# A hybrid decoder layer on one core: the first FFN's norm factor from a row-wise second copy of x

## The chip, the core and the metric

The kernel runs on one core of a Trainium2 chip. The metric is the device time of one execution in microseconds. Four compute engines work side by side, each through its own program in order, and wait for each other on semaphores: TensorE (PE: matmuls into PSUM banks), ScalarE (ACT), VectorE (DVE) and GpSimd (POOL). SyncE (SP) issues most loads, POOL issues the loads that add onto what lies in SBUF already, and both kinds run on the same 16 DMA engines. [...]

## The reference

One layer on x of 512 tokens by 1024 features, fp32: a SwiGLU FFN with RMSNorm, a token mixer, a second FFN, a gated embedding and a last norm. The change touches the norm of the first FFN alone:

```python
def rmsnorm(x, g):
    xf = x.astype(jnp.float32)
    y = xf * lax.rsqrt(jnp.mean(xf * xf, axis=-1, keepdims=True) + EPS)
    return (y * g.astype(jnp.float32)).astype(x.dtype)

h = h + 0.5 * swiglu(rmsnorm(h, ffn1_norm[i]), ffn1_w_gate[i], ffn1_w_up[i], ffn1_w_down[i])
```

The factor `rsqrt(mean(x*x) + EPS)` is one number per token. The kernel multiplies x by the gain alone before the matmuls and applies the factor, called `r`, to the products.

## The kernel before

**Layout and precision.** x is kept with features on partitions: eight tiles `h[d]` of 128 features by 512 tokens. Every fp32 operand is split in two: `hi` is a cast on ACT (L424), `lo` is the operand less `hi` on DVE (L428), and each product takes three matmul passes, hi·hi, hi·lo and lo·hi (L199 to L201, or L624 with 256 columns).

**Steps.** The program is a list of steps. Each has a weight load on SP (`load`, up to six steps ahead), a `split` of that weight two steps ahead, a `product` on PE and `after` work behind the product. `run` walks the list and writes each engine's order; `also(step, what, fn)` appends work at one of these places. Where a step is `urgent`, the `after` work of the step one before comes ahead of the split, otherwise behind it. PE, ACT, DVE and SP keep the order written; POOL's order follows the same text.

**The entry.** Steps 0 and 1 project the layer embedding, and its eight result tiles are stored to DRAM by POOL (L870), two of them pairs in buffers of the tag `rawd`. Steps 2 to 5 are the four plain steps of group 0 of the FFN: "gate, upper", "up, upper", "gate, lower", "up, lower", 24 matmuls of 512 columns each. From step 6 on, groups 1 to 10 use a Strassen-like scheme with seven products of weight and x combinations (steps "1, 7, 2, 6, 4, 5, 3" in group 1, with down-projection steps between them). Its x combinations are made by the class `Early`: `x` forms the scaled x halves and splits them, `t(both, i)` forms combination i in 3, 2, 4 and splits it, `t1` forms the last (subtraction on DVE at L535 into `embt`, cast on ACT at L537, `lo` on POOL at L539). Its weight combinations come from accumulating loads on POOL (L639, L642, L676) and one add on DVE (L634).

**The norm.** `squares` squares each `h[d]` on ACT (L247, L250), POOL adds the eight squares into `ssum` (L251), eight matmuls of one column each against ones sum over partitions into a PSUM bank with tokens on partitions (L261, behind the product of "gate, lower"). On DVE `rsqrt` (L217 to L222) and `diagonals` (L281 to L285) turn the sums into two diagonal matrices, and two matmuls against ones (L298, behind "up, lower") spread the factor over all partitions. ACT keeps the result, `r` (L304), and `plain_gate` multiplies the gate by it (DVE L728) and applies Silu (ACT L729). In group 1, `seed` copies x-products to another bank on ACT (L738), `keep_p7` and `keep_u2` copy banks on ACT (L742, L746), `plain_finish` ends group 0 (DVE L734, L735), and `gate_sum` reads banks on DVE (L756). `behind` hangs three pieces (row sums, factor with spreading, keeping) on three steps:

```python
for step, fn in zip(steps, (sums, spread, lambda: use(self.kept(got["ps"])))):
    also(step, "after", fn)
```

Where the pieces of the entry hang before the change:

```python
also(steps[1], "split", lambda: Early.x(early, 0))
also(steps[3], "split", lambda: (squares(0, 1), Early.x(early, 1), squares(2, 3)))
also(steps[4], "split", lambda: (Early.t(early, 3), squares(4, 5, 6, 7), store_embedding()))
also(steps[6], "split", lambda: Early.t(early, 2))
```

At step 7 come the Silu table load, the forming of combination 4 and `t1`, at step 9 the split of combination 4.

Of the kernel before, what the change touches and what calls it, by code (L numbers as in the profile page):

```python
# [26 lines left out]
AF = mybir.ActivationFunctionType  # L27
ALU = mybir.AluOpType

P = 128  # L30
T = 512
NC = T // P
D = 1024
# [1 line left out]
FF = 2816  # L35
NF = FF // P

G_PARTS = (1, 2, 2, 2, 2, 2)
HT = T // 2
NP = ND // 2  # L40

# [42 lines left out]
def layer_kernel(ctx: ExitStack, tc: tile.TileContext, a: dict, out: bass.AP):  # L84
    nc = tc.nc
# [69 lines left out]
    vec_warm = sb("warm", (P, 1))  # L155
    ones = sb("ones", (P, P))
# [6 lines left out]
    ps = sm_ps()  # L163
# [70 lines left out]
    class Norm:  # L234
# [77 lines left out]
        def behind(self, steps, n, use):  # L312
# [11 lines left out]
            for step, fn in zip(steps, (sums, spread, lambda: use(self.kept(got["ps"])))):  # L324
                also(step, "after", fn)


    class Step:

# [52 lines left out]
    def also(step, what, fn):  # L382

        if what == "after":
            old = step.after[0] if step.after else lambda: None
            step.after = (lambda: (old(), fn()),) + tuple(step.after[1:])
        else:
            old = getattr(step, what) or (lambda: None)
            setattr(step, what, lambda: (old(), fn()))
# [205 lines left out]
    class Group:  # L595


        def __init__(self, src, xfs, shared, j):
            self.src, self.xfs, self.shared, self.j = src, xfs, shared, j
            self.last = j == sum(G_PARTS) - 1  # L600
            self.g = self.hi = None
            self.w11, self.w12, self.w21, self.w22 = (
                Parts(tag) for tag in ("rawb", "rawb", "raw", "raw")
            )
            self.ps = {}
# [81 lines left out]
            s.from_right = i in (1, 2, 7)  # L687
            return s

        def plain_steps(self):  # L690


            def step(w, i, which, lower):
                w_parts = {}

                def split():
                    w_parts[0] = w.split()

                def product():
                    whi, wlo = w_parts[0]  # L700
                    if not lower:
                        self.ps[which] = (
                            [sm_ps(), sm_ps()] if which == "gate" else [bank("mm", 3), acc_ps()]
                        )
                    for m, ps in enumerate(self.ps[which]):
                        for p, xf in enumerate(self.xfs):
                            c = slice((2 * p + m) * P, (2 * p + m + 1) * P)
                            t = (xf.a, xf.b)[lower]
                            passes(
                                by_half(ps), whi[:, c], wlo[:, c], t[:, 0:2, 0], t[:, 0:2, 1],  # L710
                                not lower and p == 0, lower and p == len(self.xfs) - 1,
                            )

                s = Step(product, lambda: self.load((w, i)), None, split, urgent=lower)
                s.from_right = w is self.w12
                return s

            return [
                step(*s) for s in (
                    (self.w21, 2, "gate", False), (self.w11, 0, "up", False), (self.w22, 3, "gate", True), (self.w12, 1, "up", True),  # L720
                )
            ]
# [65 lines left out]
    def swiglu(name, xfs, norm, closed, after, at):  # L788


        shared = {}
        out_norm = Norm()
        src = a[f"{name}_gu"]
        groups = [Group(src[j], xfs, shared, j) for j in range(sum(G_PARTS))]
        gs = [g.steps() if g.j else None for g in groups]

        def down(part, gs_, i, n, last):

            nf = 2 * len(gs_)
            w = Parts("rawd")  # L800
            ds = D_ORDER[i * n : (i + 1) * n]
            ps = {}

            def product(gs_=gs_, first=0, end=None):
                end = len(gs_) if end is None else end
                x = [t for g in gs_[first:end] for t in g.out]
                for k, d in enumerate(ds):
                    if first == 0:
                        ps[d] = sm_ps()
                    accumulate(  # L810
                        ps[d], (w.hi, w.lo), k * nf + 2 * first, x, first == 0, end == len(gs_)
                    )

            def add():
                for d in ds:
                    nc.vector.scalar_tensor_tensor(h[d], ps[d], 0.5, h[d], ALU.mult, ALU.add)  # L816
                if last:
                    for d in ds:
                        after(d)

            def add_norm():
                if last:
                    for d in ds:
                        out_norm.add(h[d])

            step = Step(
                product, lambda: w.load(a[f"{name}_down_{part}"][:, i], n * nf * P), None,
                lambda: w.split(x="x" if (i == 1 if last else part + i) else ""), (add, add_norm),
            )
            if last and i == 0:  # L830
                step.product = lambda: product(end=len(gs_) - 1)
                step.rest = lambda: product(first=len(gs_) - 1)
            return step

        steps = groups[0].plain_steps()
        g0, pending = 0, []
        for part, n in enumerate(G_PARTS):
            if part:
                for j in range(g0, g0 + n):

                    here = pending[: -(-len(pending) // (g0 + n - j))]
                    pending = pending[len(here) :]
                    for i in (1, 7, 2, 6, 4, 5, 3) if j == 1 else (1, 7, 6, 4, 5, 2, 3):
                        steps.append(gs[j][i])
                        if i in ((5, 3 if at else 4) if j == 1 else (7, 5)):
                            steps.append(here.pop(0))
            g0 += n
            last = part == len(G_PARTS) - 1
            each = 2
            mine = groups[g0 - n : g0]  # L850
            pending = [down(part, mine, i, each, last) for i in range(ND // each)]
        steps += pending


        norm.behind(steps[at:], D, lambda r: (shared.update(r=r), groups[0].plain_gate()))
        if at:
            also(steps[8], "split", groups[0].plain_finish)
        else:
            also(steps[3], "after", groups[0].plain_finish)
        also(steps[6 if at else 4], "after", lambda: groups[0].parts_of_g(slice(0, 2)))  # L860
        also(gs[-1][3], "after", closed)
        return steps, out_norm
# [5 lines left out]
    def store_embedding():  # L868
        for to, t in stores:
            nc.gpsimd.dma_start(to, t)  # L870
# [47 lines left out]
    h = [sb("h") for _ in range(ND)]  # L918
    pad(base, "sb")
    x_ffn1, x_mix = [], []  # L920

    ffn1_norm = Norm()
    steps, mix_norm = swiglu(
        "ffn1", x_ffn1, ffn1_norm, lambda: open_region("left", "mix_left"),
        splitter("mix_norm", x_mix), 1,
# [1 line left out]
    steps = [embedding(q) for q in range(2)] + steps  # L927
    for d in range(NP):
        XForms(x_ffn1)
    early = [Early(x_ffn1[d].both_a, x_ffn1[d].both_b, d, "ffn1_norm") for d in (0, 2)]  # L930

    def load_x(*ds):
        for d in ds:
            nc.sync.dma_start(h[d], a["x"][:, d, :])

    def squares(*ds):
        for d in ds:
            ffn1_norm.add(h[d])

    also(steps[1], "load", lambda: load_x(0, 1, 2, 3))  # L940
    also(steps[3], "load", lambda: load_x(4, 5, 6, 7))

    also(steps[1], "split", lambda: Early.x(early, 0))
    also(steps[3], "split", lambda: (squares(0, 1), Early.x(early, 1), squares(2, 3)))
    also(steps[4], "split", lambda: (Early.t(early, 3), squares(4, 5, 6, 7), store_embedding()))
    also(steps[6], "split", lambda: Early.t(early, 2))

    also(
        steps[7], "split",
        lambda: (  # L950
            nc.scalar.activation(vec_warm, ones[:, 0:1], AF.Silu), Early.form(early, 4), Early.t1(early),
        ),
    )
    also(steps[9], "split", lambda: Early.t(early, 4, True))
    ffn1_steps = steps


# [3 lines left out]
    x = x_mix  # L961
# [743 lines left out]
def _laid_out(i):  # L1705
# [5 lines left out]
    def feature_major(m):  # L1711
        return np.ascontiguousarray(m.T.reshape(-1, P, m.shape[0]).transpose(1, 0, 2))

    def units(w):
# [5 lines left out]
    o = {  # L1720
        "x": feature_major(one["x"][0]),
        "p": feature_major(one["p"][0]),
    }
    cols = []
    for name, w in _VECS:
# [18 lines left out]
    for n in ("ffn1", "ffn2"):  # L1744
        o[f"{n}_gu"] = blocks(one[f"{n}_w_up"], one[f"{n}_w_gate"])
        d = units(one[f"{n}_w_down"]).reshape(ND, P, NF, P)[list(D_ORDER)]
        f0 = 0
        for q, g in enumerate(G_PARTS):
            nf = 2 * g
            o[f"{n}_down_{q}"] = np.ascontiguousarray(  # L1750
                d[:, :, f0 : f0 + nf].reshape(ND // 2, 2, P, nf * P).transpose(2, 0, 1, 3).reshape(P, ND // 2, -1)
            )
            f0 += nf
# [39 lines left out]
```

## Time and profile before

| | us |
|---|---|
| median of 3 runs (lowest, highest) | 1093.42 (1093.2, 1093.77) |
| the profiled execution | 1094.19 |
| its span | 1092.5 |
| granted clock of TensorE, mean | 0.996 |

The profile's page gives busy time by engine, and further views give the waits of an engine (waiting line, what ended the wait, total, times, longest), the timeline (start, duration, engine, line, operation, output and inputs) and windows (busy time of PE, weight load, DVE, ACT and POOL, then the granted clock of PE, the busy share of the DMA engines and GB/s). DMA rows give a queue's packets, MB and share of the 16 engines, or an issue's size and the time to its landing. q1 is the queue that SP fills, q0 that of POOL. Times are from the span's start; the first 70 us are the entry.

### The profile page before, as it was taken

What the parts mean: (1) busy time and instruction counts of PE and PEld (TensorE: products, weight loads), DVE (VectorE), ACT (ScalarE), POOL (GpSimd) and SP (SyncE); (2) the same over time, 40 slices, a digit from 0 to 9 for tenths busy, and PEclk for the clock granted to TensorE, in tenths of its full rate; (3) what the DMA queues carried; (4) which work ended last, traced back from release to release, by engine and by line L of the source; (5) the groups of instructions that cost most, each with busy time, mean ns of one, the idle gap of its engine ahead of it and who ended that gap; (6) DMA issues with size and microseconds to landing.
All of it is one profiled execution on the core that took longest, in us unless ns stands there. A gap on an engine that the chain in (4) does not pass through costs nothing.

```text
span 1092.5 us, 16566 instructions
## 1 busy us (share of the span) xinstructions
PE 1073.4 (98%) x6687; PEld 949.0 (87%) x6687; DVE 781.8 (72%) x1078; ACT 520.2 (48%) x715; POOL 153.4 (14%) x139
## 2 busy tenths in 40 slices
PE   9889999999999999999999999999999999999997
PEld 7789999999998788787878888899999999999886
DVE  7797776676667696766987766678766776767766
ACT  6554343444444455474673343454444344344554
POOL 3401000000000300134223000000000000000311
PEclk9999999999999999999999999999999999999999
DMA  9759766675624233444332333567766766643412
GB/s 362 200 140 238 195 154 180 174 193 138 182 50 134 75 93 106 135 136 135 101 112 78 97 97 107 181 155 213 202 156 184 193 179 188 161 129 100 142 50 78
DMA packets 49037, 161.67 MB, mean 148 GB/s; under 512 B 5568, under 2 KB 5824, under 8 KB 48960
## 3 DMA queue, kind: packets, MB, share of 16 engines
q1 hardware_dynamic: 38288, 124.80, 33.9%
q0 software_dynamic: 9232, 33.56, 17.2%
q10 hardware_dynamic: 1440, 2.26, 0.7%
q8 instruction: 52, 0.85, 0.3%
q14 instruction: 25, 0.20, 0.1%
HBM read 156.33 MB, written 4.26 MB: 147 GB/s over the span
## 4 chain that ended last, share of the span: by engine, by line
PE 86%; DVE 7%; ACT 4%; issue 2%; DMA 1%; SPq 0%; POOL 0%; DVEq 0%; ACTq 0%; POOLq 0%
PE mm L624 19%; PE a L624 14%; PE sm L200 10%; PE sm L199 10%; PE sm L201 10%; PE mm L200 4%; PE mm L199 4%; PE mm L201 4%; PE a L199 3%; PE a L201 3%; PE a L200 3%; DVE wlo L428 2%; ACT whi L424 1%; DVE tmp L1620 1%; DMA h<-in_x 1%
## 5 line engine op out<-in xcount | busy, mean ns | idle before, releaser
L424 ACT CAST whi<-raw 128x1024 fp32r<-128x1024 f32 x138 | 144.3, 1046 | 160.4 <-issue 60.5
L428 DVE TENSOR_TENSOR wlo<-raw,whi 128x1024 fp32r<-128x1024 f32 x137 | 172.7, 1260 | 62.4 <-ACT whi L424 61.0
L624 PE MATMUL mm<-xfb,whi 128*128 128x256 f32 x960 | 166.6, 276 | 1.6 <-ACT a L738 1.6
L624 PEld LDWEIGHTS mm<-xfb,whi 128*128 128x128 f32 x960 | 145.9, 188 | 3.4 <-ACT a L738 1.8
L624 PE MATMUL mm<-xfb,wlo 128*128 128x256 f32 x480 | 133.0, 277 | 0.3 <-DVE wlo L428 0.3
L201 PE MATMUL sm<-ghi,wlox 128*128 128x512 f32 x296 | 116.3, 393 | 0.0
L200 PE MATMUL sm<-glo,whix 128*128 128x512 f32 x296 | 115.8, 391 | 0.0
L199 PE MATMUL sm<-ghi,whix 128*128 128x512 f32 x296 | 115.1, 389 | 0.0
L624 PE MATMUL a<-xfb,whi 128*128 128x256 f32 x640 | 111.2, 276 | 1.0 <-DVE g L756 1.0
L624 PEld LDWEIGHTS a<-xfb,whi 128*128 128x128 f32 x640 | 97.7, 188 | 3.2 <-issue 1.6
L624 PEld LDWEIGHTS mm<-xfb,wlo 128*128 128x128 f32 x480 | 90.1, 188 | 0.7 <-DVE wlo L428 0.7
L624 PE MATMUL a<-xfb,wlo 128*128 128x256 f32 x320 | 88.6, 277 | 1.1 <-DVE wlo L428 1.1
L428 DVE TENSOR_TENSOR wlox<-rawd,whix 128x1024 fp32r<-128x1024 f32 (+1 forms) x40 | 45.6, 1141 | 58.7 <-ACT whix L424 58.7
L428 DVE TENSOR_TENSOR wlo<-rawb,whi 128x1024 fp32r<-128x1024 f32 x52 | 64.7, 1246 | 25.1 <-ACT whi L424 24.9
L762 ACT ACTIVATE g<-g 128x512 f32<-128x512 f32 x40 | 25.3, 632 | 108.8 <-DVE g L761 108.8
L639 POOL DMA_DIRECT2D raw<-in_ffn_gu x20 | 17.2, 860 | 387.1 <-DVE h L816 141.8
L251 POOL TENSOR_TENSOR ssum<-ssum,tmp 128x512 f32<-128x512 f32 x33 | 49.9, 1514 | 127.0 <-ACT tmp L250 126.1
L816 DVE SCALAR_TENSOR_TENSOR h<-sm,h 128x512 f32<-128x512 f32 x96 | 63.2, 683 | 5.4 <-PE sm L201 4.7
L424 ACT CAST whi<-rawb 128x1024 fp32r<-128x1024 f32 x52 | 54.2, 1043 | 26.7 <-DVE rawb L634 20.0
L201 PEld LDWEIGHTS sm<-ghi,wlox 128*128 128x128 f32 x296 | 55.5, 188 | 11.7
L200 PEld LDWEIGHTS sm<-glo,whix 128*128 128x128 f32 x296 | 55.5, 188 | 10.9
L199 PEld LDWEIGHTS sm<-ghi,whix 128*128 128x128 f32 x296 | 55.6, 188 | 10.8 <-DVE h L816 0.2
(412 smaller groups left out, 2530.8 us busy)
## 6 DMA issues: line engine op xcount, KB each, us to landing
raw<-in_ffn_gu SPq DMA_DIRECT2D x56, 512.0 KB, 5.9
rawd<-in_ffn_down SPq DMA_DIRECT2D x40, 512.0 KB, 4.0
rawb<-in_ffn_gu SPq DMA_DIRECT2D x32, 512.0 KB, 5.1
raw<-in_ffn_gu POOLq DMA_DIRECT2D x30, 512.0 KB, 5.5
raw<-in_w_in SPq DMA_DIRECT2D x29, 512.0 KB, 3.6
s<-in_ffn_gu SPq DMA_DIRECT2D x20, 512.0 KB, 6.5
s<-in_ffn_gu POOLq DMA_DIRECT2D x20, 512.0 KB, 8.7
raw<-in_w_out SPq DMA_DIRECT2D x16, 512.0 KB, 3.7
```

What stands on the lines that cost most here:

```text
L199: nc.tensor.matmul(ps, whi, xhi, start=first, stop=False)
L200: nc.tensor.matmul(ps, whi, xlo, start=False, stop=False)
L201: nc.tensor.matmul(ps, wlo, xhi, start=False, stop=last)
L251: self.engines[i].tensor_tensor(self.totals[i], self.totals[i], sq, ALU.add)
L424: nc.scalar.copy(self.hi[:, : self.n], self.raw[:, : self.n])
L428: nc.vector.tensor_tensor(self.lo[:, :n], self.raw[:, :n], self.hi[:, :n].bitcast(F32), ALU.subtract)
L624: nc.tensor.matmul(o, wt[:, c], xt, start=fresh and p == m == n == 0, stop=last and n == 2, skip_group_check=True,)
L639: nc.gpsimd.dma_start(w21.raw, self.src[0], accum_op=ALU.add)
L762: nc.scalar.activation(t, t, AF.Silu)
L816: nc.vector.scalar_tensor_tensor(h[d], ps[d], 0.5, h[d], ALU.mult, ALU.add)
L1620: engine.tensor_tensor(t, t, emb[d][:, tok], ALU.mult)
```

## The change

x is given a second time as `x_rows`, four chunks of 128 tokens on partitions by 1024 features. SP loads them at step 8, behind that step's weight load, into the buffers `whix`, `wlox`, `g` and the second of `s1`, which have other users later. ACT squares each chunk in place and sums along the row in the same instruction, so that the sums of squares come out with tokens on partitions, in SBUF. The eight Squares, seven POOL adds and eight row-sum matmuls go. The factor's work on DVE and its spreading both hang behind "up, lower"; `r` is kept one step later as before. Step 5 ("up, lower" of this FFN) is no longer urgent, so the next splits come ahead of `r`.

The other edits move work of the entry: combinations 3 and 2 of `Early` follow each other at step 4, 4 is formed and split at step 5, `t1` hangs at step 6, the first three sums at step 5, the fourth at step 6, the Silu table stays at step 7. On ACT the order behind the cast for "up, lower" is now: three row sums, two casts of combination 4, the cast for step 6, the fourth row sum, two casts of `t1`, the cast for step 7, the Silu table, the cast for step 8, `r`, Silu. On DVE: the split for "up, lower", combination 4, the split for step 6, `t1`, the factor, the splits for steps 7 and 8, the add at L634, the gate. POOL's five stores of the embedding and first two accumulating loads follow each other without adds between them. The matmuls themselves are the same. `G_PARTS` is renamed `G_6TS`.

```diff
+    class RowNorm(Norm):
+        def __init__(self, src, *tags):
+            self.src, self.tags = src, tags
+            self.rows = {}
+
+        def load(self, *chunks):
+            for c in chunks:
+                self.rows[c] = sb(self.tags[c], (P, D))
+                nc.sync.dma_start(self.rows[c], self.src[c])
+
+        def add(self, *chunks):
+            if 0 in chunks:
+                self.squares = sb("rtok", (P, NC))
+            for c in chunks:
+                t = self.rows[c]
+                nc.scalar.activation(t, t, AF.Square, accum_out=self.squares[:, c : c + 1])
+
+        def behind(self, steps, n, use):
+            got = {}
+
+            def factor():
+                got["diags"] = self.diagonals(self.of_sums(self.squares, n))
+
+            def spread():
+                got["ps"] = self.spread(got["diags"])
+
+            for step, fn in zip(steps, (factor, spread, lambda: use(self.kept(got["ps"])))):
+                also(step, "after", fn)
...
-                s = Step(product, lambda: self.load((w, i)), None, split, urgent=lower)
+                s = Step(product, lambda: self.load((w, i)), None, split, urgent=lower and not (first and w is self.w12))
...
-        norm.behind(steps[at:], D, lambda r: (shared.update(r=r), groups[0].plain_gate()))
+        norm.behind([steps[i] for i in (2, 2, 3)] if at else steps, D, lambda r: (shared.update(r=r), groups[0].plain_gate()))
...
-    ffn1_norm = Norm()
+    ffn1_norm = RowNorm(a["x_rows"], "whix", "wlox", "g", "s1")
...
+    also(steps[8], "load", lambda: ffn1_norm.load(*(0, 1, 2)))
+    also(steps[8], "load", lambda: ffn1_norm.load(*(3,)))
...
-    also(steps[3], "split", lambda: (squares(0, 1), Early.x(early, 1), squares(2, 3)))
-    also(steps[4], "split", lambda: (Early.t(early, 3), squares(4, 5, 6, 7), store_embedding()))
-    also(steps[6], "split", lambda: Early.t(early, 2))
...
-    also(steps[9], "split", lambda: Early.t(early, 4, True))
+    also(steps[3], "split", lambda: Early.x(early, 1))
+    also(steps[4], "split", store_embedding)
+    also(steps[4], "split", lambda: Early.t(early, 3))
+    also(steps[4], "split", lambda: Early.t(early, 2))
+    also(steps[5], "split", lambda: ffn1_norm.add(0, 1, 2))
+    also(steps[6], "split", lambda: ffn1_norm.add(3))
+
+    also(steps[7], "split", lambda: nc.scalar.activation(vec_warm, ones[:, 0:1], AF.Silu))
+    also(steps[5], "split", lambda: Early.form(early, 4))
+    also(steps[6], "split", lambda: Early.t1(early))
+    also(steps[5], "split", lambda: Early.t(early, 4, True))
...
+        "x_rows": np.ascontiguousarray(one["x"][0].reshape(NC, P, D)),
```

More of the change, by code (lines that the diff above doesn't have):

```diff
@@ L36 @@
 NF = FF // P
-G_PARTS = (1, 2, 2, 2, 2, 2)
+G_6TS = (1, 2, 2, 2, 2, 2)
 HT = T // 2
@@ L599, in __init__ @@
             self.src, self.xfs, self.shared, self.j = src, xfs, shared, j
-            self.last = j == sum(G_PARTS) - 1
+            self.last = j == sum(G_6TS) - 1
             self.g = self.hi = None
@@ L688, in step, with plain_steps @@
             return s
-        def plain_steps(self):
+        def plain_steps(self, first):
             def step(w, i, which, lower):
@@ L793, in swiglu @@
         src = a[f"{name}_gu"]
-        groups = [Group(src[j], xfs, shared, j) for j in range(sum(G_PARTS))]
+        groups = [Group(src[j], xfs, shared, j) for j in range(sum(G_6TS))]
         gs = [g.steps() if g.j else None for g in groups]
@@ L833, in down @@
             return step
-        steps = groups[0].plain_steps()
+        steps = groups[0].plain_steps(at)
         g0, pending = 0, []
-        for part, n in enumerate(G_PARTS):
+        for part, n in enumerate(G_6TS):
             if part:
@@ L847, in swiglu @@
             g0 += n
-            last = part == len(G_PARTS) - 1
+            last = part == len(G_6TS) - 1
             each = 2
@@ L934, in load_x @@
             nc.sync.dma_start(h[d], a["x"][:, d, :])
-    def squares(*ds):
-        for d in ds:
-            ffn1_norm.add(h[d])
     also(steps[1], "load", lambda: load_x(0, 1, 2, 3))
     also(steps[3], "load", lambda: load_x(4, 5, 6, 7))
+    also(steps[8], "load", lambda: ffn1_norm.load(*(0, 1, 2)))
+    also(steps[8], "load", lambda: ffn1_norm.load(*(3,)))
     also(steps[1], "split", lambda: Early.x(early, 0))
-    also(steps[3], "split", lambda: (squares(0, 1), Early.x(early, 1), squares(2, 3)))
-    also(steps[4], "split", lambda: (Early.t(early, 3), squares(4, 5, 6, 7), store_embedding()))
-    also(steps[6], "split", lambda: Early.t(early, 2))
[L948 to L953, printed above, removed]
-    also(steps[9], "split", lambda: Early.t(early, 4, True))
+    also(steps[3], "split", lambda: Early.x(early, 1))
[8 more added lines that the diff above has]
+    also(steps[5], "split", lambda: Early.t(early, 4, True))
     ffn1_steps = steps
@@ L1747, in _laid_out @@
         f0 = 0
-        for q, g in enumerate(G_PARTS):
+        for q, g in enumerate(G_6TS):
             nf = 2 * g
```

## The prediction

> **What bounds the kernel now.** I read the page first: busy time, then the queues' shares, then the waits of TensorE, the timeline of the entry and the DMA windows.
>
> ```profile
> PE 1073.4 (98%) x6687; PEld 949.0 (87%) x6687; DVE 781.8 (72%) x1078; ACT 520.2 (48%) x715; POOL 153.4 (14%) x139
> ```
>
> PE does nearly everything there is, so only its idle places can pay, and the change touches those of the first 70 us. Waits of PE there:
>
> ```profile
> PE mm L624 <- ACT a L738: 1.6, 1, 1.6
> PE sm L261 <- POOL ssum L251: 1.5, 1, 1.5
> PE a L624 <- ACT u L746: 1.0, 1, 1.0
> PE a L624 <- DVE g L756: 1.0, 1, 1.0
> PE a L624 <- DVE wlo L428: 0.8, 1, 0.8
> PE mm L624 <- DVE wlo L428: 0.3, 1, 0.3
> ```
>
> Where these stand on PE (start, duration, last column the wait):
>
> ```profile
> 34.68 0.40 PE L201 MATMUL sm<-xfb,wlo 128*128 128x512 f32 x1
> 36.61 1.05 PE L261 MATMUL sm<-ones,ssum 128*128 128x1 f32 x8 [1.54 <-POOL ssum L251]
> 37.53 0.48 PE L199 MATMUL mm<-xfb,whi 128*128 128x512 f32 x1
> 43.20 0.62 PE L298 MATMUL sm<-tmp,onesr 128*128 128x512 f32 x2
> 43.66 0.39 PE L624 MATMUL mm<-xfa,whi 128*128 128x256 f32 x2
> 69.00 0.47 PE L624 MATMUL a<-xfb,whi 128*128 128x256 f32 x2 [0.99 <-DVE g L756]
> ```
>
> The 24 matmuls of a step of 512 columns take 43.20-37.53 = 5.7 us, 0.23 each, so without row sums the "up, lower" step could start at 34.9 instead of 37.53: 2.6 us. The other 4.7 us (1.6+0.3+0.8+1.0+1.0) are waits for the factor's consumers on ACT and DVE. After 69 us PE runs nearly unbroken, so I carry what is won or lost at 69.00 to the end unchanged.
>
> **What goes.** Eight Squares on ACT, seven adds on POOL, eight row-sum matmuls with the 1.54 us wait. The adds also hold up DVE:
>
> ```profile
> L250 ACT ACTIVATE tmp<-h x7: 614/625/633, 16.2 to 30.3; 128x512 f32<-128x512 f32 x7
> 22.07 3.27 POOL L251 TENSOR_TENSOR ssum<-ssum,tmp 128x512 f32<-128x512 f32 x2 [2.56 <-ACT tmp L250]
> 24.37 2.05 DVE L428 TENSOR_TENSOR wlo<-raw,whi 128x1024 fp32r<-128x1024 f32 x1 [0.35 <-ACT whi L424]
> ```
>
> This split began while the second add still ran and took 2.05 us; the same split without one takes 1.22 (42.66, below). That relief comes before 37 us, where DVE then waits for something later, so I price it at nothing.
>
> **What is added: four loads of 512 KB and when they land.** SP issues them right behind the last weight load of the entry, the one at 15.92, and they run in that queue (q1). POOL's queue (q0) meanwhile carries two stores of the embedding, then two accumulating loads, which now go out 1 to 2 us earlier since no adds precede them.
>
> ```profile
> 15.92 0.43 SPq L408 DMA_DIRECT2D rawb<-in_ffn_gu  x1
> rawb<-in_ffn_gu SPq DMA_DIRECT2D x1, 512.0 KB, 11.5
> 25.83 0.91 POOL L639 DMA_DIRECT2D raw<-in_ffn_gu  x1
> 26.39 1.26 POOL L642 DMA_DIRECT2D s<-in_ffn_gu  x1
> ```
>
> Queues in four windows: 14 to 19 us, 19 to 24.5 (two rows), 24.5 to 27, and 30 to 33 us:
>
> ```profile
> q1 hardware_dynamic: 668, 2.04, 104.6%
> ...
> q1 hardware_dynamic: 340, 1.25, 55.5%
> q0 software_dynamic: 304, 1.05, 46.9%
> ...
> q1 hardware_dynamic: 217, 0.76, 74.6%
> ...
> q0 software_dynamic: 167, 0.62, 104.5%
> ```
>
> Plain loads alone move 0.41 MB/us. With both queues loaded they share packet for packet (340 to 304). Accumulating loads fill the engines at 0.21 MB/us. At 24.5 q1 still has 0.76 MB of weights; behind them come the rows. Up to the third row that is 0.76+1.57 = 2.33 MB, 5.7 us alone. Served one for one, as many packets of q0 go between them, which is all it has: stores 1.05 MB, 2.6 us, accumulations 1.05 MB, 5.1 us. So 24.5+5.7+7.7 = 37.9, and 1.0 us from the last packet to landing (weights: packets until 0.76/0.41 = 1.9 us after 24.5, landed at 15.92+11.5 = 27.4): the third row lands at **L = 38.9**. Bounds: 31.2 if the rows go first (24.5+5.7+1.0), about 41 if start-up gaps of the accumulations add. I take 38.9 because sharing is what the nearest window shows.
>
> **What waits for the rows.** ACT works in program order: cast for "up, lower", three Square sums, two xfb casts, the cast for group 1's first step, the fourth sum. It reaches the sums well before 38.9:
>
> ```profile
> 30.82 1.98 ACT L424 CAST whi<-rawb 128x1024 fp32r<-128x1024 f32 x2
> 37.14 0.62 ACT L549 CAST xfb<-ghi 128x512 fp32r<-128x512 f32 x1 [4.34 <-DVE ghi L566]
> 48.18 1.23 ACT L729 ACTIVATE g<-g 128x512 f32<-128x512 f32 x2 [0.76 <-DVE g L728]
> 50.25 0.58 ACT L738 COPY a<-mm 128x512 f32<-128x512 f32 x1
> ```
>
> No row shows a Square of 1024 with a sum: two of 512 (0.63 each) bound it above at 1.25, a 1024 cast (1.98/2) below; an extra read of the sum may add up to 0.2; I take 1.2. Two xfb casts (0.62) and one 1024 cast (0.99) take 2.2. Behind them DVE splits (1.2), forms t1 (two subtractions) and only then starts the factor:
>
> ```profile
> 39.00 0.15 DVE L217 TENSOR_SCALAR nv<-sm 128x4 f32<-128x4 f32 x1
> 42.66 1.22 DVE L428 TENSOR_TENSOR wlo<-raw,whi 128x1024 fp32r<-128x1024 f32 x1
> 45.00 1.28 DVE L535 TENSOR_TENSOR embt<-ghi 128x512 f32<-128x512 f32 x2
> 47.45 1.29 DVE L728 TENSOR_TENSOR g<-sm,rall 128x512 f32<-128x512 f32 x2 [1.17 <-ACT rall L304]
> 57.84 0.69 DVE L734 TENSOR_TENSOR g<-g,rall 128x512 f32<-128x512 f32 x1
> ```
>
> Chain start: L+1.2+2.2+1.2+1.2 = L+5.8 (0.1 of overlap) = 44.7, before 39.00. PE finishes "up, lower" at 34.9+5.7 = 40.6 and needs the diagonals, 3.7 us behind the chain's start (42.66-39.00): the wait of 1.54 us on POOL becomes one of about 8 us on ACT. Behind it PE has all of group 1. But DVE set the pace there, and it now runs its splits back to back. From chain start to the g at L734 it needs 3.7 for the factor, 3.4 for two splits and one add, then 6.2 from the g at L728: 2.0 to the end of the second Silu (47.45 to 49.41), the seed copy 0.6, a cast 1.0, the copy of p7 0.5, a cast 1.0, a split 1.2 (the other split runs under ACT). In all 13.3 us, before 57.84-39.00 = 18.8, since the splits then waited for ACT. L734 falls at L+19.1 = 58.0, before 57.84, and the g at L756, which PE awaits at 69.00, follows at the same distance. So the edit shifts 69.00 by L-38.8 = **+0.1**.
>
> Two costs stand on top. First, t1's two adds on POOL now run beside the factor chain:
>
> ```profile
> L539 POOL TENSOR_TENSOR xfa<-embt,xfa x2: 1392/1398/1405, 46.4 to 47.7; 128x512 fp32r<-128x512 f32 x2
> L221 DVE SCALAR_TENSOR_TENSOR nt<-nt,nv x27: 161/161/1151, 39.6 to 1080.3; 128x4 f32<-128x4 f32 x24, 128x2 f32<-128x2 f32 x3
> ```
>
> One of the chain's small operations took 1.15 instead of 0.16 us where POOL worked. Two POOL operations, 1.0 each: **+2.0** (bounds 0 and 2.8, twice 1.40). The Trainium skill (SBUF — State Buffer, Who interferes with whom) says that a DVE instruction with two SBUF inputs and a GpSimd one that reads SBUF exclude each other for the whole instruction; by it this term would be 2.8, by the row 2.0.
>
> Second, an idle PE loses its clock (PEclk is the column behind POOL):
>
> ```profile
> 551.00:553.00 2.00, 0.37 (x2) 0.00 (x0) 1.86 (x7) 1.96 (x7) 0.64 (x1) 1.00 0.66 210
> 553.00:555.00 2.00, 1.01 (x14) 0.80 (x16) 0.78 (x2) 2.00 (x4) 0.00 (x0) 1.00 0.37 150
> 555.00:557.00 2.00, 2.00 (x21) 1.67 (x17) 0.86 (x2) 2.00 (x4) 1.27 (x1) 0.55 0.00 0
> 557.00:560.00 3.00, 3.00 (x10) 2.44 (x11) 3.00 (x6) 1.96 (x3) 0.00 (x0) 0.73 0.00 0
> ```
>
> After 2.6 us idle in four, 2x0.45+3x0.27 = 1.7 us of clock were lost. An idle 8 us or more should do the same once. PE resumes L624 at L+9.9+2.0 = 50.8 and needs 25.3 us less 4.7 of waits (and up to 1.0 of refill) to the place of 69.00, so it has up to 0.7 us to spare behind DVE: **+1.0** shows (bounds 0, 3.4 for two such periods). [...]
>
> At nothing: SP's later loads (rawd waited for the stores anyway; s1 now waits for the fourth Square, but is needed for group 2, behind 69 us); the moved casts of xfb forms, on an idle ACT and DVE before 31 us; the fill of q1, which is not the path after 50 us. If that cover went, 1 us each.
>
> **Sum.** 0.1+2.0+1.0 = +3.1 on the profiled 1094.19 is 1097.3; the median shown is 0.77 lower: **1096.5**.
>
> **Rivals.** (1) Rows late, but nothing on top, the POOL adds slipping into gaps and the clock holding: +0.1, 1093.5; for it, most small operations show no stall; against it, POOL starts just then. (2) The other side: the rows are served ahead of the accumulations, L = 31.2. The chain starts at 37.0, diagonals stand at 42.7 with the stall, L624 at 43.2; PE gains 0.5 there and the 4.7 us of waits: -5.2, 1088.2. For it: from 24.5 to 27 q1 held three quarters of the engines; against it, the even sharing before that, and that accumulations are issued before the first row can start. It decides below L = 34.6, where 2.0+L-38.8 passes -2.2. (3) Rows at 41 and a second half-clock period: +5.5, 1098.9.
>
> **Numbers.** What a measurement of this kernel can tell from no change is about 0.2%, 2.2 us. Forecast 0.50, rival 3 0.07, rival 1 0.18, rival 2 0.25. Slower 0.57, same 0.18, faster 0.25. Both signs hold much, so the range reaches from 1089.2, inside rival 2, to 1098.9; the forecast's own is 1095 to 1098.5.
>
> **What will show it.** Right: the four loads of x_rows land between 31 and 41, the third near 39; ACT idles on DMA before the second and third Square; PE waits 7 to 10 us ahead of L298, on DVE; granted clock near 0.55 behind it; the waits at a, u and wlo gone. Wrong: if the third Square starts before 34 us, or L298 before 44 us.

## The result, and the profile after

| | before | after |
|---|---|---|
| median, us (runs) | 1093.6 (4) | 1098.85 (4) |
| the profiled execution, us | 1094.19 | 1099.35 |
| its span, us | 1092.5 | 1097.6 |
| step 3 of group 1 starts on PE, us | 69.00 | 74.03 |

The change makes the kernel slower: the ratio is 1.0046, with a 95% interval of 1.0034 to 1.0058. From the start of step 3 to the end of the span both kernels take the same 1023.5 us (1092.5-69.00, 1097.6-74.03 = 1023.6), so all of it lies in the entry.

Waits of PE up to 80 us in the changed kernel:

```profile
PE sm L298 <- DVE tmp L285: 9.9, 1, 9.9
PE sm L165 <- DVE tmp L162: 1.7, 1, 1.7
PE a L653 <- DVE g L785: 0.9, 1, 0.9
PE sm L199 <- ACT whi L924: 0.8, 1, 0.8
```

The row-sum wait and the waits at `a`, `u` and `wlo` of before are gone (one at `g`, L756 there and L785 here, stays). Those at L165 and L199 lie in the first 7 us and were there before (1.7 and 0.3). In place of the others stands one wait of 9.9 us for the diagonals. ACT's timeline (start, duration, last column the wait) shows where it begins:

```profile
34.64 1.06 ACT L342 ACTIVATE whix<-whix 128x1024 f32<-128x1024 f32 x1 [5.43 <-DMA whix<-in_x_rows]
35.61 0.19 ACT L342 ACTIVATION_READ_ACCUMULATOR whix<-whix 128x1 f32 x1
38.40 1.06 ACT L342 ACTIVATE wlox<-wlox 128x1024 f32<-128x1024 f32 x1 [2.60 <-DMA wlox<-in_x_rows]
40.02 1.06 ACT L342 ACTIVATE g<-g 128x1024 f32<-128x1024 f32 x1 [0.48 <-DMA g<-in_x_rows]
59.50 0.59 ACT L771 COPY p<-mm 128x512 f32<-128x512 f32 x1 [1.19 <-PE mm L653]
67.59 1.05 ACT L453 CAST whi<-rawb 128x1024 fp32r<-128x1024 f32 x1 [0.56 <-ACT whi L453]
```

ACT is ready for the sums at 29.2 and stands idle for the rows, 5.43, 2.60 and 0.48 us. The last two rows come back below. DVE and POOL behind it:

```profile
41.72 0.69 DVE L580 TENSOR_TENSOR xfb<-ghi,xfb 128x512 fp32r<-128x512 f32 x1 [10.04 <-ACT xfb L578]
45.53 0.16 DVE L217 TENSOR_SCALAR nv<-rtok 128x4 f32<-128x4 f32 x1
45.93 1.11 DVE L220 TENSOR_TENSOR nt<-ny 128x4 f32<-128x4 f32 x1
47.07 1.19 DVE L221 SCALAR_TENSOR_TENSOR nt<-nt,nv 128x4 f32<-128x4 f32 x1
51.16 1.22 DVE L457 TENSOR_TENSOR wlo<-raw,whi 128x1024 fp32r<-128x1024 f32 x1
62.21 0.69 DVE L763 TENSOR_TENSOR g<-g,rall 128x512 f32<-128x512 f32 x1
...
45.74 2.50 POOL L568 TENSOR_TENSOR xfa<-embt,xfa 128x512 fp32r<-128x512 f32 x2 [19.82 <-ACT xfa L566]
```

DVE waits 10.04 us for an xfb cast that does not need the rows: it is only queued behind three Squares on ACT. Then the factor's chain starts at 45.53, and two of its operations on four columns take 1.11 and 1.19 us while POOL runs t1's two adds (45.74 to 48.24). PE resumes:

```profile
50.70 1.40 PE L298 MATMUL sm<-tmp,onesr 128*128 128x512 f32 x2 [9.86 <-DVE tmp L285]
74.03 0.47 PE L653 MATMUL a<-xfb,whi 128*128 128x256 f32 x2 [0.88 <-DVE g L785]
```

and does so at half clock, as two windows show (PE busy in the second column, its granted clock behind POOL):

```profile
40.00:46.00 6.00, 0.83 (x4) 0.35 (x2) 4.04 (x8) 5.09 (x9) 0.26 (x1) 0.98 0.60 222
46.00:56.00 10.00, 5.30 (x22) 4.89 (x23) 9.51 (x18) 4.98 (x8) 3.92 (x4) 0.50 0.73 158
```

5.30 us of PE at 0.50 are 2.65 us of work lost. Last, the queues from 24.5 to 33 us, and the third row's load (KB, time to landing):

```profile
q0 software_dynamic: 393, 1.48, 55.5%
q1 hardware_dynamic: 445, 1.63, 48.0%
...
g<-in_x_rows SPq DMA_DIRECT2D x1, 512.0 KB, 21.5
```

The rows share the engines with POOL's queue nearly packet for packet, 445 to 393; issued at 18.52, the third row lands at 40.0.

### The profile page after: what moved, and what is told of

Read it like the earlier page. It is cut to its first block, busy times and chain, and to the rows that moved or that the text cites. A ratio compares the mean times of both kernels' runs of the same rounds, so it can differ in the third digit from the quotient of the medians.

```text
span 1097.6 us, 16536 instructions
## 1 busy us (share of the span) xinstructions
PE 1072.7 (98%) x6679; PEld 948.6 (86%) x6679; DVE 780.4 (71%) x1078; ACT 520.5 (47%) x715; POOL 141.4 (13%) x132
## 4 chain that ended last, share of the span: by engine, by line
PE 85%; DVE 6%; DMA 4%; ACT 3%; issue 1%; DVEq 0%; ACTq 0%
PE mm L653 19%; PE a L653 14%; PE sm L200 10%; PE sm L199 10%; PE sm L201 10%; PE mm L200 4%; PE mm L199 4%; PE mm L201 4%; PE a L199 3%; PE a L201 2%; PE a L200 2%; DMA g<-in_x_rows 2%; DVE wlo L457 1%; ACT whi L453 1%; DMA rawb<-in_ffn_gu 1%
## 5 line engine op out<-in xcount | busy, mean ns | idle before, releaser
L199 PE MATMUL sm<-ghi,whix 128*128 128x512 f32 x296 | 115.3, 390 | 0.0
L199 PEld LDWEIGHTS sm<-ghi,whix 128*128 128x128 f32 x296 | 55.6, 188 | 11.1 <-DVE h L845 0.4
L653 PEld LDWEIGHTS a<-xfb,wlo 128*128 128x128 f32 x320 | 60.1, 188 | 0.5 <-DVE wlo L457 0.5
```

Of the source, the lines that this page charges most:

```text
L199: nc.tensor.matmul(ps, whi, xhi, start=first, stop=False)
L653: nc.tensor.matmul(o, wt[:, c], xt, start=fresh and p == m == n == 0, stop=last and n == 2, skip_group_check=True,)
```

## The experiments

The theory after this reading: the rows land late because POOL's accumulating loads share the DMA engines; ACT's program order puts work that needs no rows behind them; the late chain meets POOL's adds; PE, idle for 9.9 us, restarts at half clock. Rivals: the moved work of the entry carries the loss, or the new order on ACT and DVE does so whenever the rows land. The runs stand in one table, but for three first tries (rows_first, lo_behind_factor, pe_warm), which are told beside their second versions; the times of the columns are from each kernel's profile. Each ratio is to the runs of the kernel before that were taken beside it, whose medians lie between 1093.5 and 1093.9.

| kernel | third Square | chain start | L298 | wait of PE there | step 3 | median, us | ratio to before (95%) |
|---|---|---|---|---|---|---|---|
| before | - | 39.00 | 43.20 | 0 | 69.00 | 1093.6 | |
| the change | 40.02 | 45.53 | 50.70 | 9.9 | 74.03 | 1098.85 | 1.0046 (1.0034-1.0058) |
| no_rows | - | 36.93 | 40.64 | 0 | 65.14 | 1089.62 | 0.9962 (0.9950-0.9974) |
| rows_first2 | 34.58 | 40.09 | 45.27 | 4.5 | 67.76 | 1094.07 | 1.0000 (0.9990-1.0009) |
| lo_behind_factor2 | 39.59 | 45.10 | 48.30 | 7.3 | 71.44 | 1096.88 | 1.0027 (1.0018-1.0036) |
| pe_warm2 | 39.6 | 45.13 | 50.43 | 0.8 | 72.06 | 1097.59 | 1.0034 (1.0021-1.0047) |
| sums_after_t1 | 39.43 | 41.91 | 45.11 | 4.4 | 68.71 | 1094.11 | 1.0002 (0.9993-1.0011) |
| moves_alone | - | 41.78 | 45.00 | 2.7 | 69.89 | 1093.41 | 0.9996 (0.9987-1.0005) |
| late_sums_345 | 43.58 | 45.79 | 48.99 | 2.9 | 67.29 | 1092.88 | 0.9988 (0.9979-0.9997) |
| late_sums_b | 40.91 | 43.11 | 46.33 | 0.2 | 66.68 | 1092.22 | 0.9983 (0.9974-0.9991) |
| late_sums_c | 40.75 | 42.96 | 46.17 | 0 | 64.12 | 1089.74 | 0.9968 (0.9956-0.9980) |

**no_rows: the rows' arrival taken away.**

```diff
-                nc.sync.dma_start(self.rows[c], self.src[c])
...
-                nc.scalar.activation(t, t, AF.Square, accum_out=self.squares[:, c : c + 1])
+                nc.scalar.activation(
+                    t.rearrange("p (k t) -> p k t", k=2), h[2 * c].unsqueeze(1).to_broadcast([P, 2, T]),
+                    AF.Square, accum_out=self.squares[:, c : c + 1],
+                )
```

> The four row loads are left out; each Square reads a tile of x that is already in SBUF (twice over, 1024 elements), so r is not the reference's. Theory (ACT's queue stands behind rows that land late): ACT runs the sums from 29 us, chain start 45.5 -> about 37, L298 50.7 -> about 42.5, PE waits under 2.5 us ahead of it, clock stays at 1.0, step 3 of group 1 at 64 to 66 instead of 74.0; time 1088.5 to 1091. Rival (the new order on ACT and DVE, or POOL's adds in the chain, and not the arrival): L298 within 2 us of 50.7 and time at least 1097.

Measured 1089.62, chain start 36.93, L298 at 40.64, 2 us ahead of the 42.5 expected, since the chain no longer meets POOL's adds. Step 3 at 65.14. The order of the change is the same here, so the order alone does not cost: the rows and what is queued behind them do, 9.2 us against the changed kernel. One thing came otherwise than expected: the clock did not stay at 1.0. PE waited 1.97 us for a copy of ACT until 48.69, and its clock fell behind that wait:

```profile
50.00:52.00 2.00, 2.00 (x11) 2.00 (x11) 1.79 (x2) 1.04 (x2) 0.83 (x1) 0.50 0.17 35
```

**rows_first2: the accumulating loads behind the rows.** A first try (rows_first) put a POOL copy of a row's element ahead of them. POOL's program did not keep that order, although the text ahead says that POOL follows what is written (the first loads still went out at 23.74 and 25.24, the copy waited by itself until 41.27), so nothing was delayed, and a second effect came in with it (below). In the second, a zero formed from the fourth row is added to each target's first column, which the load must wait for:

```diff
+        row = ffn1_norm.rows[3][:, 0:1]
+        nc.gpsimd.tensor_tensor(vec_warm, row, row, ALU.subtract)
+        for raw, src in acc_later:
+            nc.gpsimd.tensor_tensor(raw[:, 0:1], raw[:, 0:1], vec_warm, ALU.add)
+            nc.gpsimd.dma_start(raw, src, accum_op=ALU.add)
```

> POOL's first two accumulating loads now really stand behind the fourth row (each target's first column gets an added zero that is formed from that row). Theory (the rows are late because they share the DMA engines with the accumulations): third Square 40.0 -> about 34, fourth row about 35, chain start about 39.4, L298 about 44.6, step 3 at about 68, time 1092 to 1094. Rival (the rows are late because of the weights and stores ahead of them): third Square not before 38 and no gain. Second rival (the delayed accumulations become the new wait, at the cast of step 7 or the add of step 6): third Square at 34 but step 3 after 71, time above 1096.

Queues from 24.5 to 33 us, the third row's load, and the third Square:

```profile
q1 hardware_dynamic: 681, 2.48, 71.7%
q0 software_dynamic: 292, 1.05, 30.2%
...
g<-in_x_rows SPq DMA_DIRECT2D x1, 512.0 KB, 15.8
...
34.58 1.06 ACT L342 ACTIVATE g<-g 128x1024 f32<-128x1024 f32 x1
```

q1 moves 681 packets in the same 8.5 us where it moved 445, the third row lands 15.8 instead of 21.5 us behind its issue, and the third Square comes 5.44 us earlier. The chain and L298 follow by 5.44 and 5.43, step 3 by 6.27, the time by 4.8, to that of before. So 5.4 us of the rows' lateness are the accumulating loads' doing, and nine tenths of that (4.8 of 5.4) reach the end.

**lo_behind_factor2: t1's adds on POOL away from the chain.** The first try (lo_behind_factor) had the same fault as rows_first: the adds still ran at 45.11, inside the chain. The second adds a zero formed from the second diagonal to one column of the adds' input:

```diff
+            diag = ffn1_norm.got["diags"][1][:, 0:1].bitcast(F32)
+            nc.gpsimd.tensor_tensor(vec_warm, diag, diag, ALU.subtract)
             for n, e in enumerate(both):
+                one = f[:, n, 0, 0:1]
+                nc.gpsimd.tensor_tensor(one, one, vec_warm, ALU.add)
                 nc.gpsimd.tensor_tensor(e.a[:, 1, 1], f[:, n], e.a[:, 1, 0].bitcast(F32), ALU.subtract)
```

> POOL's two adds of t1 now really wait for the second diagonal (a zero formed from it is added to one column of their input). Theory (the adds block two small DVE operations of the chain): chain start stays at 45.5, chain to diagonals 2.0 shorter, L298 50.7 -> 48.7, step 3 at 72.0, time 1096.9 (-2.0). Rival (the adds then block DVE's splits as much): L298 48.7, but the splits at L457 behind it take 2 us or more and step 3 is within 0.5 of 74.0, time 1098.4 to 1099. Rival (the adds come too late for product 7): PE waits for xfa, over 1 us, and no gain.

The two operations, without POOL beside them:

```profile
45.50 0.16 DVE L220 TENSOR_TENSOR nt<-ny 128x4 f32<-128x4 f32 x1
45.70 0.16 DVE L221 SCALAR_TENSOR_TENSOR nt<-nt,nv 128x4 f32<-128x4 f32 x1
```

0.16 us each instead of 1.11 and 1.19. The time falls by 1.97 us (1098.85 to 1096.88): the stall is real, worth what it was priced at, and on the path. In the profiled execution L298 comes 2.40 us earlier, 0.43 of it because the third Square stands 0.43 us earlier there.

**pe_warm2: the clock.** The first try (pe_warm) used 40 matmuls on an x tile that t1 still writes:

```profile
45.78 11.78 PE L353 MATMUL sm<-xfa,onesr 128*128 128x512 f32 x40 [5.23 <-ACT xfa L569]
```

They waited for t1's casts and held L298 back until 57.4, 6.7 us later than in the changed kernel, which made 1102.86 us: a fault of the experiment, which tells nothing of the clock. The second uses constants:

```diff
             def spread():
-                got["ps"] = self.spread(got["diags"])
+                ps = sm_ps()
+                for _ in range(40):
+                    nc.tensor.matmul(
+                        ps.rearrange("p (c t) -> p c t", c=NC), ones_r,
+                        ones_r.unsqueeze(1).to_broadcast([P, NC, P]), start=True, stop=True,
+                    )
+                got["ps"] = self.spread(got["diags"], ps)
```

> 40 matmuls of 512 columns on constants, into the bank of L298, stand ahead of L298; their result is overwritten. Theory (the idle PE loses its clock, 2.6 us of PE work, of which the seed's and p7's waits for PE, 0.26 and 1.19, are on the path): they run from 40.8 to about 50, granted clock 1.0 from 42 to 56, both ACT waits on PE gone, step 3 about 1.5 earlier at 72.6, time 1097.4. Rival (the loss is hidden behind DVE and ACT): clock 1.0 and step 3 within 0.4 of 74.0, time 1098.5 to 1099.2. Rival (all PE work lost is on the path): step 3 at 71.4, time 1096.2.

```profile
46.00:50.00 4.00, 3.62 (x16) 2.65 (x15) 3.66 (x12) 3.31 (x4) 3.58 (x4) 1.00 0.39 99
...
40.37 9.25 PE L353 MATMUL sm<-onesr 128*128 128x512 f32 x40
50.43 1.10 PE L298 MATMUL sm<-tmp,onesr 128*128 128x512 f32 x2 [0.81 <-DVE tmp L285]
72.06 0.47 PE L659 MATMUL a<-xfb,whi 128*128 128x256 f32 x2 [0.76 <-DVE g L791]
...
65.62 1.05 ACT L459 CAST whi<-rawb 128x1024 fp32r<-128x1024 f32 x1 [0.49 <-PE mm L659]
```

The clock stays at 1.00, and ACT's waits for PE at the seed and at p7 vanish; a third one, at the cast in the last row, stays at 0.49. The median falls by 1.26 us, to 1097.59. (Its profiled execution took 1099.4, the four others 1097.4 to 1097.9; up to step 3 it shows nothing odd.) The intervals of the two ratios overlap, so the trace has to carry the reading: from chain start to the g of group 0 it takes 15.19 us (45.13 to 60.32) instead of 16.68 (45.53 to 62.21), which is 1.49 less: the two waits that vanished were 1.45. About half of the 2.65 us of lost PE work was on the path.

**sums_after_t1: only the place of the Squares on ACT.**

```diff
-    also(steps[5], "split", lambda: ffn1_norm.add(0, 1, 2))
-    also(steps[6], "split", lambda: ffn1_norm.add(3))
...
     also(steps[6], "split", lambda: Early.t1(early))
+    also(steps[6], "split", lambda: ffn1_norm.add(0, 1, 2, 3))
```

> Only the place of the four Squares on ACT differs from the changed kernel: behind t1's casts. Theory (the late rows cost because split and t1 are queued behind the Squares): third Square still near 40, chain start 45.5 -> 42.5 (three us), POOL's adds done before 40, so chain to diagonals 2.0 shorter, L298 50.7 -> 45.7, PE wait near 4.9, step 3 at 69, time 1093.8 (-5). Rival (the rows' landing alone sets the start of the chain): chain start within 0.7 of 45.5, time over 1096.

The third Square stays near 40 (39.43), yet the chain starts at 41.91, 3.6 us earlier, and runs unslowed; L298 comes at 45.11, the time is 1094.11. So the rows' landing costs mainly through what the program had put behind the Squares, and the place of four instructions is worth 4.7 us. That is not to be added to the 4.8 us of rows_first2: each takes back nearly the whole loss of 5.25, by the same chain. PE still waits 4.4 us here, and its clock is 0.50 from 46 to 50 us.

**moves_alone: the moved work of the entry with the norm of before.**

```diff
-    also(steps[4], "split", lambda: (Early.t(early, 3), squares(4, 5, 6, 7), store_embedding()))
-    also(steps[6], "split", lambda: Early.t(early, 2))
+    also(steps[4], "split", lambda: (store_embedding(), Early.t(early, 3), squares(4, 5, 6, 7), Early.t(early, 2)))
...
+    also(steps[5], "split", lambda: Early.form(early, 4))
+    also(steps[6], "split", lambda: Early.t1(early))
+    also(steps[5], "split", lambda: Early.t(early, 4, True))
```

> The kernel before with its own norm (Squares of x, POOL adds, row sums on PE); only the moved work of the entry is as in the change (combinations 3, 2, 4 at steps 4 and 5, t1 at step 6, stores first). Theory (the moves cost nothing by themselves but put POOL's t1 adds beside the factor chain, +2.0 at L298, and take up to 4 us of later waits away): L298 at 44 to 46, step 3 at 66.5 to 69.5, time 1091 to 1094. Rival (the moves carry the loss): L298 after 48 or step 3 after 71, time over 1096.

The time is that of before (ratio 0.9996). L298 is 1.8 us later, as expected, but by another way: the chain itself is unslowed and starts at 41.78, behind a split and t1's subtractions that now precede it on DVE. Behind it PE waits 2.67 us and runs at a clock of 0.65 from 46 to 50 us, and step 3 comes 0.9 us later than before in the profiled execution (which took 1095.09, the median 1093.41). In the time, the moves carry none of the loss.

**late_sums_345, late_sums_b, late_sums_c: towards a version that gains.** All three keep the loads and hang the factor behind step 1 of group 1, the spreading behind its step 7 and `r` behind its step 2, so that PE has two more steps to do before it needs the diagonals. They differ in what stands where:

```diff
-    also(steps[5], "split", lambda: ffn1_norm.add(0, 1, 2))
-    also(steps[6], "split", lambda: ffn1_norm.add(3))
+    also(steps[8], "split", lambda: ffn1_norm.add(0, 1, 2, 3))
...
-        norm.behind([steps[i] for i in (2, 2, 3)] if at else steps, D, lambda r: (shared.update(r=r), groups[0].plain_gate()))
+        norm.behind([steps[i] for i in (3, 4, 5)] if at else steps, D, lambda r: (shared.update(r=r), groups[0].plain_gate()))
```

That is late_sums_345. late_sums_b changes this to

```diff
-    also(steps[8], "split", lambda: ffn1_norm.add(0, 1, 2, 3))
+    also(steps[7], "split", lambda: ffn1_norm.add(0, 1, 2, 3))
...
-                s = Step(product, lambda: self.load((w, i)), None, split, urgent=lower and not (first and w is self.w12))
+                s = Step(product, lambda: self.load((w, i)), None, split, urgent=lower)
```

and late_sums_c adds to late_sums_b

```diff
+    add6, steps[9].sums = steps[9].sums, None
+    also(steps[7], "split", add6)
```

> Same loads and same work as the changed kernel; the four Squares stand on ACT behind the casts for steps 7 and 8, the factor hangs behind step 1 of group 1, the spreading behind its step 7, r behind its step 2. Theory (the rows are late, and the loss comes from what is queued behind the Squares on ACT and from PE's order, not from the rows as such): third Square near 41, chain start near 43.5, t1's POOL adds before 38 and out of the chain, PE waits under 1 us ahead of L298, clock 1.0, step 3 at 63 to 65.5, time 1088 to 1090.5. Rival (whoever loads the rows here pays: later r moves the wait to the gate, the g at L763 and the finish of group 0): PE waits over 3 us at the a or g of group 1, time 1093 to 1097.

It is 1 us faster than before, where 3 to 6 were expected:

```profile
40.53 1.05 ACT L453 CAST whi<-rawb 128x1024 fp32r<-128x1024 f32 x1 [1.51 <-issue]
...
48.99 1.39 PE L298 MATMUL sm<-tmp,onesr 128*128 128x512 f32 x2 [2.85 <-DVE tmp L285]
...
48.00:50.00 2.00, 1.01 (x2) 0.69 (x3) 1.97 (x5) 0.00 (x0) 0.00 (x0) 0.59 1.02 250
50.00:52.00 2.00, 2.00 (x10) 1.91 (x10) 1.63 (x3) 0.82 (x2) 0.00 (x0) 0.50 1.00 412
```

The cast for step 8, ahead of the Squares, waited until 40.53, so the chain started at 45.79 instead of 43.5, PE stood idle for 2.85 us, and that was enough to halve its clock.

> As the version with late sums, but the four Squares stand on ACT behind the cast for step 7 and ahead of that for step 8, and the factor stands on DVE ahead of the split for step 8 (step 5 is urgent again). Theory (in late_sums_345 the cast for step 8 held the Squares until 41.5 although two rows had landed, so the diagonals came 2.85 us after PE was out of work, and the idle halved the clock): third Square 43.6 -> about 40.9, chain start 45.8 -> 42.5, PE waits under 0.5 us ahead of L298, clock 1.0 throughout, step 3 67.3 -> 63 to 64.5, time 1089 to 1090.5. Rival (ACT and DVE set the pace behind the factor whatever PE does): PE wait gone, but step 3 not before 66, time 1091.5 to 1093.

PE's wait and the clock loss are gone as the theory had it, but step 3 comes at 66.68 and the time is 1092.22: the rival's numbers. One cast of ACT waited, while DVE had been idle before the chain:

```profile
49.23 1.05 ACT L453 CAST whi<-rawb 128x1024 fp32r<-128x1024 f32 x1 [4.73 <-DVE rawb L663]
...
43.11 0.17 DVE L217 TENSOR_SCALAR nv<-rtok 128x4 f32<-128x4 f32 x1 [3.59 <-ACT s L342]
```

> As late_sums_b, but the add at L663 stands on DVE ahead of the factor instead of behind the diagonals and the split for step 8. Theory (in late_sums_b the cast for step 6 waited 4.73 us for that add, while DVE had stood idle 3.59 us for the last Square before it): add at 39.5 to 40.7, that cast at about 44.5 instead of 49.23, PE's waits at wlo and u together under 1.5 us instead of 3.5, step 3 66.7 -> 64 to 65, time 1089.5 to 1090.8. Rival (the g chain behind r sets step 3 whatever this add does): step 3 within 0.7 of 66.7, time 1091.6 to 1092.5.

```profile
39.25 1.21 DVE L663 TENSOR_TENSOR rawb<-rawb,s 128x1024 f32<-128x1024 f32 x1
...
44.28 1.05 ACT L453 CAST whi<-rawb 128x1024 fp32r<-128x1024 f32 x1
...
64.12 0.48 PE L653 MATMUL a<-xfb,whi 128*128 128x256 f32 x2 [0.91 <-DVE g L785]
```

As expected: the add fills DVE's gap, the cast comes 4.95 us earlier, step 3 at 64.12, time 1089.74. This version is 0.32% (0.20 to 0.44%) faster than the kernel before, beats both, and with all four rows loaded it is as fast as the changed kernel without them (no_rows).

## Why the prediction was right, and where its sizes were off

The direction, the place and the mechanisms held; the shift was 5.03 us at step 3 (5.25 between the medians) where +3.1 was forecast. The 1098.85 lies outside the forecast's own 1095 to 1098.5, at the very edge of the wide range (1098.9). That it meets the number of rival 3 is luck. The terms of that rival, as stated, make 2.2 for rows at 41, 2.0 for the adds and 3.4-0.7 = 2.7 for two half-clock periods, 6.9 and not 5.5, and neither of its conditions came about in full: the third row landed at 40.0, and 2.65 us of PE work were lost, between the 1.7 of one period and the 3.4 of two. By the forecast's own steps:

- **What is won or lost at 69.00 reaches the end unchanged.** Right: 1023.5 and 1023.6 us behind it.
- **L, the landing of the third row, 38.9.** Off by 1.1: 40.0. One-for-one sharing is what the queues show, and rows_first2 shows that it is the cause. Where the missing 1.1 us lies in the queue was not tried.
- **Chain start at L+5.8.** It is L+5.5 (40.02, 45.53): a Square with its sum costs ACT 1.06 us (40.02 to the cast at 41.08), not 1.2; the read of the sum, 0.19, overlaps.
- **13.3 us from chain start to the g at L734 (now L763).** Without stalls it holds: 62.21-45.53 is 16.68, less 1.97 of stall and 1.45 of ACT's waits for PE (0.26 at the seed, 1.19 at p7) leaves 13.26. So the edit term was +0.95 (chain +6.53, regained 18.84-13.26 = 5.58), not +0.1: the later L less the shorter Square.
- **+2.0 for POOL's adds.** Right: from chain start to the split behind the diagonals 5.63 us (45.53 to 51.16) instead of 3.66, and -1.97 in the time when they are moved away. The rule of the Trainium skill (SBUF — State Buffer, Who interferes with whom) agrees in kind: each of the two operations ended when a POOL add did. Its 2.8, from a longer add, was too much: the pair took 2.50 here, and had begun before the first stalled operation.
- **+1.0 for the clock.** Too small, the mis-sized term. The forecast lost 1.7 us once and left PE 0.7 us to spare; 2.65 us were lost, and ACT waited for PE in three places: 0.26, 1.19, and 0.56 at the cast at 67.59, behind which the way from g to step 3 takes 0.66 more than before (74.03-62.21 = 11.82, 69.00-57.84 = 11.16). The profile names the cast before as what ended that last wait; in pe_warm2 it names a matmul for the same cast, and it starts as PE ends the product ahead, so I read it as a buffer that PE frees late (not tried). Together 2.1 us. Only part of that is the clock: in pe_warm2, at a clock of 1.00, the first two waits are gone (1.49 at the g, 1.26 in the time), but the way from g to step 3 still takes 11.74 (60.32 to 72.06). So 0.6 of the 0.66 is not the clock's doing. That PE is late there because L298 is as late as in the changed kernel (50.43) is likely, but not shown; the forecast has no term for it.
- 0.95+1.97+1.45+0.66 = 5.03: of the 1.93 missing, 0.85 is the edit term (the rows' landing, less the shorter Square), 1.1 PE's late and slow restart.
- **At nothing.** Right for the moved work: moves_alone is at 0.9996. Pricing the relief of DVE from POOL's eight-square adds at nothing fits too: DVE then waited 10.04 us.
- **Rival 1 (nothing on top).** Both costs on top came, the stall and the clock.
- **Rival 2 (rows ahead of the accumulations).** rows_first2 made it so, with L = 34.6, the point from which it should have counted as faster by 2.2; it came out even. What the rival left out is that a wait of PE remains at that L, 4.5 us, and costs clock again (0.65 from 46 to 50 us, 1.4 us of work): step 3 comes only 1.24 us before that of before. Behind step 3 it takes 0.6 us more than before (1091.9-67.76 = 1024.1), which was not followed; over the kernels of the table that stretch takes 1023.5 to 1024.1, and 1025.6 in the profiled execution of pe_warm2.
- **What was to show it.** The third row near 39, ACT idle on DMA before the Squares, a wait of 7 to 10 us on DVE ahead of L298, a clock near 0.55 behind it: 40.0, yes, 9.9, 0.50. The fourth row landed at 41.3 (20.14+21.2), just behind the 41 that was given for all four.

## What to carry to other kernels

A load that is issued early is not early data: price its landing by what shares the engines, and in an in-order engine put the instruction that waits for it behind all that does not need it. Here the same loads cost 5.25 us or gained 3.9, by the place of four Squares, one add and the factor. A wait that is moved to the matmul engine can also cost the clock of the work behind it; here it did from a wait of 1.97 us on, and not at 1.61.

## What the runs showed of the hardware that was not expected

**With one extra tile of 4 bytes per partition, the kernel took 20 us more.** rows_first and lo_behind_factor each allocate one extra tile of one column, the target of a POOL copy:

```diff
+        nc.gpsimd.tensor_copy(sb("gate1", (P, 1)), ffn1_norm.rows[3][:, 0:1])
```

Both took 1118 us (1118.35 and 1118.12, ratio 1.022), with the entry of the changed kernel and no new wait. Matmuls of 256 columns (count, then shortest, median and longest in ns), first in the changed kernel, then in these two:

```profile
L653 PE MATMUL mm<-xfb,whi x960: 274/276/287, 56.6 to 1012.5; 128*128 128x256 f32 x192
...
L653 PE MATMUL mm<-xfb,whi x960: 276/280/285, 56.3 to 1031.4; 128*128 128x256 f32 x192
...
L659 PE MATMUL mm<-xfb,whi x960: 276/280/285, 55.6 to 1030.8; 128*128 128x256 f32 x192
```

Each takes about 4 ns more, there are some 6,700 matmuls, and PE's busy time grows from 1072.7 to 1094.1 us. The second versions, which write the result of their POOL operation into a tile that is there already, do not have this. That the tile shifts the addresses of others is the likely reading; it was not tried by itself.

**Short idle times halve the clock.** 2.85 us of idle in late_sums_345 brought it to 0.50 at once, 2.67 us in moves_alone to 0.65 over the next 4 us, and 1.97 us in no_rows to 0.50 from 50 to 52 us. The wait of 1.61 us ahead of 50.88 in the kernel before left it at 1.00, and the half clock that the prediction shows at 555 us stands behind 1.87 and 0.75 us of idle with two matmuls between them. The 3.4 us that the Trainium skill (TensorE: Matmul & The Clock Gate, Part 1) gives for the idle window is thus no safe bound here.

**A split can lose the whole length of two POOL adds.** In moves_alone a split that takes 1.22 us alone ran beside t1's adds:

```profile
45.47 4.33 DVE L428 TENSOR_TENSOR wlo<-raw,whi 128x1024 fp32r<-128x1024 f32 x1
...
45.87 2.84 POOL L539 TENSOR_TENSOR xfa<-embt,xfa 128x512 fp32r<-128x512 f32 x2
```

It took 4.33 us, the sum of both (1.22+2.84 = 4.06) and 0.27 more.
